# Seven products for eight in part of the MLP's second matrix, in a two-layer encoder on one core

## The chip, the core and the metric

The kernel runs on one core of a Trainium2 chip. The engines named here are TensorE (PE; its weight loads are listed as PEld), VectorE (DVE), ScalarE (ACT), GpSimd (POOL) and SyncE (SP), which issues most of the loads. Each takes its instructions in the order of a list of its own and waits where one needs another's result. The metric is the time of an execution on the device in microseconds; lower is better.

## What is computed

Two layers, 256 tokens, model width 2048. The mixer of layer 0 is a gated linear recurrence, that of layer 1 a 2-D neighbourhood attention. The part that changes is the second product of `sqrelu_mlp`.

```python
D_MODEL = 2048
SEQ = 256
D_FF = 4 * D_MODEL

def sqrelu_mlp(h, w1, w2):
    a = jax.nn.relu(h @ w1)
    return (a * a) @ w2

    for i in range(DEPTH):
        ...
        h = h + mix
        h = h + sqrelu_mlp(rms_norm(h, norm_mlp[i]), mlp_w1[i], mlp_w2[i])
        gate = jax.nn.sigmoid(rms_norm(h, norm_ple[i]) @ ple_w_gate[i])
        h = h + gate * (p[i] @ ple_w_proj[i])
    return rms_norm(h, norm_final)
```

## The kernel before

All matrix products are in float32 made of two parts: a number is split into a high part (rounded to TensorE's fp32r format) and the remainder, its low part. A product is then three matmuls: high by high, low activation by high weight, high activation by low weight. A tile of activations holds both parts side by side, 256 tokens high and 256 low. Weights come from memory as raw f32, a quarter (512 rows by 512 columns, 1 MB) at a time, and are split on the chip in halves of 128x1024 elements (`block`): ScalarE copies the half into `wh`, VectorE subtracts and writes `wl`. `wh` and `wl` have four buffers each, raw weights three, and in the MLP and gate stages two more (`phase("mlp", 2)`). One half is a step; after each step `tick` gives a turn to work that was put off (norms, transposes of the residual stream).

The MLP of a layer goes in four rounds, `for f in range(4)`. A round takes 2048 of the 8192 hidden columns: four groups of w1 (`group`, 512 columns each, weights stationary, 8 steps of 16 matmuls), each followed by relu and square and a split into a tile of activations `acts[g]`; and then w2's four column groups (`residual`, `tgroup`, `tadd`, `tproduct`), each over the round's four quarters of w2's rows. In `tproduct` the activations are stationary and the weights move: a step is 12 matmuls of 512 columns, six for each half of the tokens (s = 0, 1), and a column group is 8 steps, 96 matmuls. `residual_add` then multiplies the product by the squared norm factor r2 and adds it into the residual h (L361); in the last round `settle` squares the new h for the next norm and transposes it for the gate stage (`turned`, `gained`).

Products accumulate in PSUM in three double banks (`mm`, 2x512 columns) and two single ones (`psm`, for transposes and small products). The order of work on an engine is fixed when the program is built: a scheduler interleaves the instructions along their dependencies, by their order in the code and its own idea of when each can start.

Low products of w1: in a `group` the low products of weights stand behind the two high ones of each 128-column tile in layer 0 (`lows` = 1), behind those of all four tiles in layer 1 (`lows` = 2), and alternate with the high ones in the attention stage (`lows` = 0).

Of the kernel before, what the change touches and what calls it, by code (L numbers as in the profile page):

```python
# [12 lines left out]
F32 = mybir.dt.float32  # L13
F32R = mybir.dt.float32r
AF = mybir.ActivationFunctionType
ALU = mybir.AluOpType
# [3 lines left out]
P = 128  # L20
D = 2048
T = 256
# [8 lines left out]
V_MIX, V_MLP, V_PLE, V_FIN, V_CW, V_CB, V_AB, V_XB, V_LAM = 0, 2, 4, 6, 7, 11, 12, 14, 16  # L31
# [2 lines left out]
AHEAD = 400  # L34
LEAD = 3
NG = D // 512


class Late:


    def __init__(self, tiles):
        self.tiles = tiles
# [8 lines left out]
class Trunk:  # L52
    def __init__(self, ctx, tc, d):
        self.tc, self.nc, self.d = tc, tc.nc, d
        nc = self.nc
        pool = lambda name, bufs, **kw: ctx.enter_context(tc.tile_pool(name=name, bufs=bufs, **kw))
        self.const = pool("const", 1)
        self.state = pool("state", 1)
        self.wraw = pool("wraw", 3)
        self.wsplit = pool("wsplit", 4)  # L60
        self.work = pool("work", 2)
        self.psum = pool("psum", 3, space=PSUM)
        self.psm = pool("psm", 2, space=PSUM)
# [10 lines left out]
        self.lows = 0  # L74

    def v(self, which, c):
        i = which * NC + c
# [82 lines left out]
    def add(self, ps, w, xs, quarters, before=None, loads=1, summed=False):  # L160
        nc = self.nc

        def lows(step, ts):
            k0, wh, wl = step
            for t in ts:
                o = ps[t // 2][:, t % 2, :]
                c = slice(t * P, (t + 1) * P)
                for k in range(2):
                    kc = k0 + k
                    nc.tensor.matmul(o[:, T:], wl[:, k, c], xs[kc][:, :T], start=False, stop=kc == len(xs) - 1)  # L170
# [61 lines left out]
    def norm_begin(self):  # L232
        self.ss = self.work.tile([P, 2, NG], F32, name="ss")

# [92 lines left out]
    def load_h(self):  # L327
        nc = self.nc
        self.x = [self.state.tile([P, 4, T], F32, name=f"x{g}", tag=f"as{g}") for g in range(4)]
        self.h = [self.state.tile([P, 2, 512], F32, name=f"h{g}") for g in range(NG)]  # L330
        self.xs = self.new_xs("xs")
        self.load_pair(0)

        def squares():
            self.norm_begin()
            for _ in range(3):
                yield
            for g in range(NG):
                nc.sync.dma_start(self.h[g], self.d["h"][:, :, 512 * g : 512 * (g + 1)])
# [119 lines left out]
    def rg_mixer(self):  # L459
        nc = self.nc  # L460
        with self.phase("rg", 0) as pool:
# [31 lines left out]
            self.xs = self.new_xs("xs")  # L493
            for g in range(NG):
                if g < LEAD:
# [99 lines left out]

    def mlp_ple(self, layer, home, other, which):

        with self.phase("mlp", 2) as pool:
            self.mlp(pool, layer, home, other)
            self.lows = 0  # L600
            self.ple(pool, layer, which, other)

    def mlp(self, pool, layer, home, other):
        nc = self.nc
        r2 = pool.tile([P, 2], F32, name="r2")
        self.lows = 1 + layer
        self.ple_load(pool, layer)
        self.norm_later(lambda r: nc.vector.tensor_tensor(r2, r, r, ALU.mult))
# [27 lines left out]
    def ple(self, pool, layer, which, home):  # L636
        nc = self.nc
        r = pool.tile([P, 2], F32, name="r_ple")
        self.norm_later(lambda tok: nc.vector.tensor_copy(r, tok))
        xs = self.xlist(self.xs)  # L640
        if which is not None:
            self.xs = self.new_xs(home)
        else:
            gain = pool.tile([P, D], F32, name="gain")
            nc.scalar.dma_start(gain, self.d["gain"])
        for g in range(NG):
            if g % 2 == 0:
                halves = self.block(self.d["proj"][layer, g // 2])
            wh, wl = (t.rearrange("p (k n) -> p k n", k=2) for t in next(halves))
            pj = pool.tile([P, 2, 512], F32, name="pj", bufs=2)  # L650
# [127 lines left out]
```

## Time and profile before

| | us |
|---|---|
| median of three runs | 2349.58 |
| lowest and highest | 2348.42 to 2349.86 |
| profiled execution | 2348.25 |
| its span, first to last instruction | 2346.2 |

The span is what the trace covers; 2.05 us of the profiled execution lie around it. The mean granted clock of TensorE in it is 0.997 of full speed. In the rows below a line begins with the start and the duration where it is from a timeline; "x2" says that two like instructions were merged, and their duration is then that of both. L107 is the subtraction of the low part, L106 the copy of the high part, L361 the addition into h, L144, L145 and L149 the three kinds of matmul in w2, L183 and L170 those of w1.

### The profile page before, as it was taken

The numbers are of one execution on the slowest core, as the hardware profiler recorded it, in microseconds if no ns is written. First come the engines' busy times: TensorE is split into PE (matmuls) and PEld (weight loads), VectorE is DVE, ScalarE is ACT, GpSimd is POOL, SyncE is SP. The second block draws the span as 40 slices with busy tenths as digits, with TensorE's granted clock in tenths as the row PEclk, the third lists the DMA queues.
The fourth block names the chain that finished last, engine by engine and source line by source line (L and its number), as shares of the span: only waits on it lengthen the run. The fifth ranks groups of instructions, "written<-read, shape, count | busy, mean of one in ns | idle before, by whom it ended". The sixth has DMA issues, their size and how long they took to land.

```text
span 2346.2 us, 30442 instructions
## 1 busy us (share of the span) xinstructions
PE 2315.7 (99%) x12356; PEld 1991.8 (85%) x12356; DVE 1420.1 (61%) x1634; ACT 1177.4 (50%) x1527; POOL 0.9 (0%) x9
## 2 busy tenths in 40 slices
PE   8999999999999999999999999999999999999997
PEld 8999888888888888888888888888888888888885
DVE  6888766556555555556676666555555555555564
ACT  7888554344344344455455545544344344344453
POOL 0000000000000000000000000000000000000000
PEclk9999999999999999999999999999999999999998
DMA  7455655555555555554555555555555555555452
GB/s 289 166 177 180 229 184 186 196 190 187 197 188 189 197 187 191 191 185 163 177 178 177 179 186 220 182 195 185 192 197 183 195 191 187 196 188 189 179 181 88
DMA packets 63947, 440.93 MB, mean 188 GB/s; under 512 B 6976, under 2 KB 7104, under 8 KB 11968
## 3 DMA queue, kind: packets, MB, share of 16 engines
q1 hardware_dynamic: 62400, 433.61, 52.2%
q10 hardware_dynamic: 1408, 5.39, 0.7%
q8 instruction: 96, 1.57, 0.3%
q14 instruction: 43, 0.35, 0.0%
HBM read 436.88 MB, written 2.10 MB: 187 GB/s over the span
## 4 chain that ended last, share of the span: by engine, by line
PE 93%; ACT 3%; DVE 3%; issue 1%; DMA 0%; SPq 0%; ACTq 0%
PE mm L183 25%; PE mm L144 16%; PE mm L145 16%; PE mm L149 16%; PE mm L170 10%; PE mm L185 3%; ACT wh L106 1%; PE mm L209 1%; PE mm L207 1%; PE mm L208 1%; DVE wl L107 1%; PE pt L296 1%; DVE ig L447 1%; ACT L226 1%; ACT m L226 1%
## 5 line engine op out<-in xcount | busy, mean ns | idle before, releaser
L107 DVE TENSOR_TENSOR wl<-raw,wh 128x1024 fp32r<-128x1024 f32 x816 | 996.7, 1223 | 786.1 <-ACT wh L106 784.0
L106 ACT CAST wh<-raw 128x1024 fp32r<-128x1024 f32 x816 | 855.3, 1050 | 1004.6 <-PE mm L145 521.7
L183 PE MATMUL mm<-as,wh 128*128 128x512 f32 x1536 | 444.0, 395 | 0.0
L144 PE MATMUL mm<-wh,as 128*128 128x512 f32 x896 | 350.4, 391 | 0.0
L145 PE MATMUL mm<-wh,as 128*128 128x512 f32 x896 | 349.1, 390 | 0.0
L183 PEld LDWEIGHTS mm<-as,wh 128*128 128x128 f32 x1536 | 278.3, 189 | 53.7
L183 PE MATMUL mm<-xs,wh 128*128 128x512 f32 x1024 | 322.1, 396 | 0.0
L144 PE MATMUL mm<-wh,xs 128*128 128x512 f32 x768 | 301.0, 392 | 0.0
L145 PE MATMUL mm<-wh,xs 128*128 128x512 f32 x768 | 299.2, 390 | 0.0
L149 PE MATMUL mm<-wl,as 128*128 128x512 f32 x896 | 241.2, 390 | 0.0
L170 PEld LDWEIGHTS mm<-xs,wl 128*128 128x128 f32 x1024 | 192.4, 188 | 45.3
L149 PE MATMUL mm<-wl,xs 128*128 128x512 f32 x768 | 205.8, 389 | 0.0
L170 PE MATMUL mm<-xs,wl 128*128 128x256 f32 x1024 | 201.2, 278 | 0.0
L144 PEld LDWEIGHTS mm<-wh,as 128*128 128x128 f32 x896 | 168.3, 188 | 34.5
L145 PEld LDWEIGHTS mm<-wh,as 128*128 128x128 f32 x896 | 168.3, 188 | 34.0
L149 PEld LDWEIGHTS mm<-wl,as 128*128 128x128 f32 x896 | 167.7, 188 | 34.4
L149 PEld LDWEIGHTS mm<-wl,xs 128*128 128x128 f32 x768 | 144.1, 188 | 30.2
L144 PEld LDWEIGHTS mm<-wh,xs 128*128 128x128 f32 x768 | 144.3, 188 | 29.4
L145 PEld LDWEIGHTS mm<-wh,xs 128*128 128x128 f32 x768 | 144.3, 188 | 29.3
L183 PEld LDWEIGHTS mm<-xs,wh 128*128 128x128 f32 x1024 | 156.3, 189 | 0.3
L170 PEld LDWEIGHTS mm<-as,wl 128*128 128x128 f32 x1024 | 144.0, 190 | 12.9
L207 PE MATMUL mm<-xs,wh 128*128 128x256 f32 x512 | 146.1, 286 | 8.3 <-ACT wh L106 7.3
(140 smaller groups left out, 2119.8 us busy)
## 6 DMA issues: line engine op xcount, KB each, us to landing
raw<-in_w SPq DMA_DIRECT2D x256, 1024.0 KB, 4.7
raw<-in_qkv SPq DMA_DIRECT2D x48, 1024.0 KB, 4.8
raw<-in_ple SPq DMA_DIRECT2D x32, 1024.0 KB, 4.7
raw<-in_w_in SPq DMA_DIRECT2D x28, 1024.0 KB, 4.8
raw<-in_w_out SPq DMA_DIRECT2D x16, 1024.0 KB, 4.8
raw<-in_na_out SPq DMA_DIRECT2D x16, 1024.0 KB, 4.8
raw<-in_w_in SPq DMA_DIRECT2D x8, 512.0 KB, 8.5
raw<-in_gates SPq DMA_DIRECT2D x4, 1024.0 KB, 4.7
```

What stands on the lines that cost most here:

```text
L106: nc.scalar.copy(wh, raw[:, c])
L107: nc.vector.tensor_tensor(wl, raw[:, c], wh.bitcast(F32), ALU.subtract)
L144: nc.tensor.matmul(ps[:, s, :], part(k, 0), wh[:, k, :], start=first and k == 0, stop=False)
L145: nc.tensor.matmul(ps[:, s, :], part(k, T), wh[:, k, :], start=False, stop=False)
L149: nc.tensor.matmul(ps[:, s, :], part(k, 0), wl[:, k, :], start=False, stop=last and k == n - 1)
L170: nc.tensor.matmul(o[:, T:], wl[:, k, c], xs[kc][:, :T], start=False, stop=kc == len(xs) - 1)
L183: nc.tensor.matmul(o, wh[:, k, c], xs[kc], start=first, stop=False)
L185: nc.tensor.matmul(o[:, T:], wl[:, k, c], xs[kc][:, :T], start=False, stop=last)
L207: nc.tensor.matmul(o, a, x[:, :T], start=first, stop=False)
L208: nc.tensor.matmul(o, a, x[:, T:], start=False, stop=False)
L209: nc.tensor.matmul(o, b, x[:, :T], start=False, stop=last)
L226: self.tc.stamp_issue_order_token(self.nc.scalar.activation(*args, **kw).ins, "table")
```

## The change

A quarter of w2's rows and a pass of two neighbouring column groups (g and g + 1) make a block of 512 rows by 1024 columns. With the rows halved (k = 0, 1), the columns halved (f = 0, 1) and the tokens halved (s = 0, 1), it is eight products of blocks. In some quarters the change makes seven, by Strassen's scheme in Winograd's form: P1, Q5, P6, Q3, P2, Q4, P7 in the code. Its factors are sums of blocks. Sums of activations are made once per quarter (`seven`: the tile d, split into b, besides the plain parts in a); sums of weights are made in each pass by VectorE, in place, in the order u += r, u += v, u += w_, v += r, where u, r, v and w_ are the four blocks of the quarter, loaded apart (512 KB each). Each sum is split again (`cut`) for its product. `SEVEN = (2, 1, 2, 1)` is the number of such quarters in the four rounds. The other quarters stay as they were (`plain`) and are put between the products by the table `SPREAD`. The results go into h in pieces (`take`): P1, Q5, P6 and P7 reach more than one block of h, through a tile t of sums.

A pass uses four double banks of PSUM where there are three: P6 and P7 come into that of P1 and Q5. The MLP phase loses the two more raw buffers and gains single tiles u_w, v_w, r_w (r_w shares its place with e of `seven`). The low products of w1 and of the attention's q and k all take the order that layer 0's w1 had. The gain vector of the last norm takes the place of xs0.

```diff
+SPREAD = {1: (2, 4, 0, 0, 0, 4, 2), 2: (2, 2, 0, 0, 0, 2, 2), 3: (1, 1, 0, 0, 0, 1, 1)}
+SEVEN = (2, 1, 2, 1)
...
-                        if not self.lows:
-                            nc.tensor.matmul(o[:, T:], wl[:, k, c], xs[kc][:, :T], start=False, stop=last)
-                if self.lows == 1:
-                    lows(step, (t,))
-            if self.lows == 2:
-                lows(step, ts)
+                if not summed:
+                    for k in range(2):
+                        kc = k0 + k
+                        nc.tensor.matmul(o[:, T:], wl[:, k, c], xs[kc][:, :T], start=False, stop=kc == len(xs) - 1)
...
-        with self.phase("mlp", 2) as pool:
+        with self.phase("mlp", 0) as pool:
...
+                if g < SEVEN[f]:
+                    acts.append(self.seven(pool, ps, f"{other}{g}", g))
+                    continue
...
-            self.residual(w, self.xlist(acts), V_PLE + layer, home, by=r2, last=f == 3)
+            if f == 3:
+                self.norm_begin()
+                self.xs = self.new_xs(home)
+            for g in range(0, NG, 2):
+                self.double(pool, w, acts, SEVEN[f], g, r2, nr2)
+                if f == 3:
+                    self.settle(g, V_PLE + layer, self.xs[g])
+                    self.settle(g + 1, V_PLE + layer, self.xs[g + 1])
+    def seven(self, pool, ps, name, g):
...
+        e = pool.tile([P, 2, 2, 2, P], F32, name="e", tag="r")
+        d = pool.tile([P, 3, 2, P], F32, name="d")
+        for i in range(2):
+            u = self.joined(ps[i], "u")
+            nc.vector.scalar_tensor_tensor(e[:, i].rearrange("p k s n -> p k (s n)"), u, 0.0, u, ALU.max, ALU.mult)
+        a11, a21, a12, a22 = (e[:, i, :, s] for i in range(2) for s in range(2))
+        nc.vector.tensor_tensor(d[:, 1], a11, a21, ALU.subtract)
+        nc.vector.tensor_tensor(a21, a21, a22, ALU.subtract)
+        nc.vector.tensor_tensor(d[:, 0], a21, a11, ALU.subtract)
+        nc.vector.tensor_tensor(d[:, 2], a12, d[:, 0], ALU.add)
+        a = self.state.tile([P, 8, T], F32R, name=name)
+        b = pool.tile([P, 6, T], F32R, name=f"b{g}")
+        for o, x in ((a, e.rearrange("p i k s n -> p (i k s) n")), (b, d.rearrange("p i k n -> p (i k) n"))):
+            nc.scalar.copy(o[:, :, :P], x)
+            nc.vector.tensor_tensor(o[:, :, P:], x, o[:, :, :P].bitcast(F32), ALU.subtract)
...
+    def cut(self, src):
...
+            nc.scalar.copy(wh, src)
+            nc.vector.tensor_tensor(wl, src, wh.bitcast(F32), ALU.subtract)
...
+    def double(self, pool, w, acts, n, g, by, nby):
...
+        for pair in ("P1", "Q5"), "YZ", "WV", ("P6", "P7"):
+            ps = self.psum.tile([P, 2, 512], F32, name="mm", tag="mm")
...
+        for q in range(n):
+            nc.sync.dma_start(u[:, q, :], wide(q, 0, 0))
+        r_ = pool.tile([P, 2, 1024], F32, name="r_w", tag="r")
+        for q in range(n):
+            nc.sync.dma_start(r_[:, q, :], wide(q, 1, 0))
+        for q in range(n):
+            nc.sync.dma_start(v[:, q, :], wide(q, 1, 1))
...
+        def one(b, a, src, stop):
+
+            wh, wl = self.cut(src)
+            for k in range(2):
+                mm(b, a[:, k, :P], wh[:, k, :])
+                mm(b, a[:, k, P:], wh[:, k, :])
+            for k in range(2):
+                mm(b, a[:, k, :P], wl[:, k, :], stop and k == 1)
...
+        def take(b, f, s, sign=1):
+            h = self.h[g + f][:, s, :]
+            r = (by if sign > 0 else nby)[:, s : s + 1]
+            nc.vector.scalar_tensor_tensor(h, bank[b] if b else t, r, h, ALU.mult, ALU.add)
...
+        order = ["P1", "Q5", "P6", "Q3", "P2", "Q4", "P7"]
+        gaps = SPREAD[n]
+        for name, m in zip(order, gaps):
+            for q in range(n):
+                a = acts[q]
+                if name == "P1":
+                    one("P1", a[0], u[:, q, :], q == n - 1)
+                    nc.vector.tensor_tensor(u[:, q, :], u[:, q, :], r_[:, q, :], add)
+                elif name == "Q3":
+                    one("W", a[6], v[:, q, :], left["W"] == 1)
+                    done("W")
+                    nc.vector.tensor_tensor(v[:, q, :], v[:, q, :], r_[:, q, :], add)
+                elif name == "Q5":
+                    one("Q5", a[1], u[:, q, :], q == n - 1)
+                    nc.vector.tensor_tensor(u[:, q, :], u[:, q, :], v[:, q, :], add)
+                elif name == "P6":
...
+                    one("P6", a[4], u[:, q, :], q == n - 1)
+                    nc.vector.tensor_tensor(u[:, q, :], u[:, q, :], w_[:, q, :], add)
+                elif name == "P2":
+                    one("Y", a[2], w_[:, q, :], left["Y"] == 1)
+                    done("Y")
+                elif name == "P7":
+                    one("P7", a[5], v[:, q, :], q == n - 1)
+                else:
+                    one("Z", a[3], u[:, q, :], left["Z"] == 1)
+                    done("Z")
+                self.tick()
...
+            some(m)
```

What stands where on the engines is shown at two places, both in w2 of the third round of layer 0, where two quarters go by seven products; the number behind a name tells one buffer from another. On VectorE before, between the additions into h of the third and the fourth column group, there are the eight splits of a column group:

```order
L361 SCALAR_TENSOR_TENSOR h2_91<-mm_7004,r2_3357,h2_91 128x512 x2
L107 TENSOR_TENSOR wl_7197<-raw_7178,wh_7196 128x1024
L107 TENSOR_TENSOR wl_7215<-raw_7212,wh_7214 128x1024
L107 TENSOR_TENSOR wl_7231<-raw_7212,wh_7230 128x1024
L107 TENSOR_TENSOR wl_7249<-raw_7246,wh_7248 128x1024
L107 TENSOR_TENSOR wl_7265<-raw_7246,wh_7264 128x1024
L107 TENSOR_TENSOR wl_7287<-raw_7284,wh_7286 128x1024
L107 TENSOR_TENSOR wl_7299<-raw_7284,wh_7298 128x1024
L107 TENSOR_TENSOR wl_7329<-raw_7326,wh_7328 128x1024
L361 SCALAR_TENSOR_TENSOR h3_92<-mm_7143,r2_3357,h3_92 128x512 x2
```

In the changed program VectorE has this, in the second pass, from the splits for P6 to those for P2 (u_w, v_w and r_w are blocks of weights, raw_7331 holds the block w_, h2 and h3 are the pass's two column groups):

```order
L661 TENSOR_TENSOR wl_7335<-u_w_7206,wh_7334 128x1024
L661 TENSOR_TENSOR wl_7346<-u_w_7206,wh_7345 128x1024
L762 TENSOR_TENSOR u_w_7206<-u_w_7206,raw_7331 128x1024 x2
L661 TENSOR_TENSOR wl_7359<-v_w_7207,wh_7358 128x1024
L661 TENSOR_TENSOR wl_7370<-v_w_7207,wh_7369 128x1024
L779 TENSOR_TENSOR t_7205<-mm_7204,t_7205 128x512
L752 TENSOR_TENSOR v_w_7207<-v_w_7207,r_w_7210 128x1024
L717 SCALAR_TENSOR_TENSOR h3_92<-t_7205,nr2_3361,h3_92 128x512
L752 TENSOR_TENSOR v_w_7207<-v_w_7207,r_w_7210 128x1024
L661 TENSOR_TENSOR wl_7381<-raw_7331,wh_7380 128x1024
L661 TENSOR_TENSOR wl_7391<-raw_7331,wh_7390 128x1024
```

Sums of weights (L762, L752) and additions (L779, L717) now stand between the splits, and two of the four sums lie ahead of the splits for P2.

On TensorE before, the fourth column group goes on step by step, low products behind the high ones of the same step:

```order
L144 MATMUL mm_7143<-wh_7162,as0_6156 128x512
L145 MATMUL mm_7143<-wh_7162,as0_6156 128x512
L149 MATMUL mm_7143<-wl_7163,as0_6156 128x512 x4
L144 MATMUL mm_7143<-wh_7180,as1_6341 128x512
L145 MATMUL mm_7143<-wh_7180,as1_6341 128x512
```

In the changed program TensorE has this in the same second pass, from P2 (as0 and as1 with wh_7380 and wh_7390) on:

```order
L688 MATMUL mm_7202<-wh_7380,as0_6319 128x512 x4
L688 MATMUL mm_7202<-wl_7381,as0_6319 128x512 x2
L688 MATMUL mm_7202<-wh_7390,as1_6511 128x512 x4
L688 MATMUL mm_7202<-wl_7391,as1_6511 128x512 x2
L688 MATMUL mm_7203<-wh_7424,as2_6687 128x512 x6
L688 MATMUL mm_7202<-wh_7401,as0_6319 128x512 x4
L688 MATMUL mm_7202<-wl_7402,as0_6319 128x512 x2
L688 MATMUL mm_7202<-wh_7411,as1_6511 128x512 x4
L688 MATMUL mm_7202<-wl_7412,as1_6511 128x512 x2
L688 MATMUL mm_7203<-wh_7424,as2_6687 128x512 x2
L688 MATMUL mm_7203<-wl_7425,as2_6687 128x512 x4
```

Six high products of the plain quarter as2 were moved ahead of Q4 (wh_7401, wh_7411), and their low ones (wl_7425) behind it.

## Rows read from the trace of the kernel before

**Rows 1.** The page's head: span, then busy time, share and instructions of each engine.

```profile
span 2346.2 us, 30442 instructions
PE 2315.7 (99%) x12356; PEld 1991.8 (85%) x12356; DVE 1420.1 (61%) x1634; ACT 1177.4 (50%) x1527; POOL 0.9 (0%) x9
```

**Rows 2.** The page's chain that ended last: share of the span by engine.

```profile
PE 93%; ACT 3%; DVE 3%; issue 1%; DMA 0%; SPq 0%; ACTq 0%
```

**Rows 3.** The list of waits: engine and line, releaser, us in total, times, longest.

```profile
DVE wl L107 <- ACT wh L106: 784.0, 632, 3.0
ACT wh L106 <- PE mm L145: 521.7, 324, 2.6
DVE h L361 <- PE mm L149: 42.2, 32, 1.3
```

**Rows 4.** VectorE's timeline, w2, layer 0's third round: start, us, instruction, idle before.

```profile
781.56 1.41 DVE L361 SCALAR_TENSOR_TENSOR h<-mm,r,h 128x512 f32<-128x512 f32 x2 [1.32 <-PE mm L149]
782.88 1.21 DVE L107 TENSOR_TENSOR wl<-raw,wh 128x1024 fp32r<-128x1024 f32 x1
...
803.32 1.41 DVE L361 SCALAR_TENSOR_TENSOR h<-mm,r,h 128x512 f32<-128x512 f32 x2 [1.32 <-PE mm L149]
```

**Rows 5.** w1, w2 of that round: PE, PEld, DVE, ACT, POOL, clock, DMA, GB/s.

```profile
670.40:759.60 89.20, 89.20 (x514) 77.84 (x513) 52.22 (x53) 39.57 (x46) 0.00 (x0) 1.00 0.53 186
759.60:846.60 87.00, 87.00 (x386) 72.09 (x385) 46.25 (x44) 35.82 (x36) 0.00 (x0) 1.00 0.56 196
```

**Rows 6.** Timeline of VectorE where it is dense, in the RG-LRU stage.

```profile
87.11 1.20 DVE L107 TENSOR_TENSOR wl<-raw,wh 128x1024 fp32r<-128x1024 f32 x1
88.23 1.22 DVE L451 TENSOR_TENSOR ig<-ig,ig 128x1024 f32<-128x1024 f32 x1
89.37 0.68 DVE L392 TENSOR_TENSOR xr<-mm,rstd 128x512 f32<-128x512 f32 x1
```

**Rows 7.** Timeline of VectorE in w1 of layer 0's third round.

```profile
736.72 0.69 DVE L221 TENSOR_TENSOR u<-mm,low 128x512 f32<-128x512 f32 x1
737.44 0.69 DVE L617 SCALAR_TENSOR_TENSOR u<-u 128x512 f32<-128x512 f32 x1
...
739.49 0.68 DVE L214 TENSOR_TENSOR as<-u,as 128x512 fp32r<-128x512 f32 x1
740.09 0.68 DVE L221 TENSOR_TENSOR u<-mm,low 128x512 f32<-128x512 f32 x1
...
759.01 0.69 DVE L221 TENSOR_TENSOR u<-mm,low 128x512 f32<-128x512 f32 x1
```

**Rows 8.** ScalarE's costliest group: instruction, count, busy us, mean ns, idle.

```profile
L106 ACT CAST wh<-raw 128x1024 fp32r<-128x1024 f32 x816 | 855.3, 1050 | 1004.6 <-PE mm L145 521.7 <-PE mm L183 354.2 <-issue 90.2
```

**Rows 9.** Timeline of TensorE where the same round goes from w1 to w2.

```profile
759.59 0.40 PE L144 MATMUL mm<-wh,as 128*128 128x512 f32 x1
```

**Rows 10.** Timeline of VectorE where a column group settles, gate stage of layer 0.

```profile
1033.11 0.48 DVE L286 SCALAR_TENSOR_TENSOR xs<-pt,vec,xs 128x256 fp32r<-128x256 f32 x1
1034.14 0.48 DVE L286 SCALAR_TENSOR_TENSOR xs<-pt,vec,xs 128x256 fp32r<-128x256 f32 x1 [0.54 <-ACT xs L285]
```

**Rows 11.** Timeline of VectorE at the ends of two w1 groups, layer 1.

```profile
1744.36 1.28 DVE L221 TENSOR_TENSOR u<-mm,low 128x512 f32<-128x512 f32 x2
...
1766.73 1.28 DVE L221 TENSOR_TENSOR u<-mm,low 128x512 f32<-128x512 f32 x2
```

**Rows 12.** Timeline of TensorE in a group of the attention stage.

```profile
1158.61 0.40 PE L183 MATMUL mm<-as,wh 128*128 128x512 f32 x1
...
1162.77 0.40 PE L183 MATMUL mm<-as,wh 128*128 128x512 f32 x1
```

**Rows 13.** DMA issues (KB each, us to landing), and SP's longest wait.

```profile
raw<-in_w SPq DMA_DIRECT2D x256, 1024.0 KB, 4.7
raw<-in_w_in SPq DMA_DIRECT2D x8, 512.0 KB, 8.5
...
SPq L99 <- DVE wl L107: 2017.0, 385, 11.2
```

More of the change, by code (lines that the diff above doesn't have):

```diff
@@ L161, in add @@
         nc = self.nc
[L163 to L170, printed above, removed]
         def tiles(step, ts):
@@ L605, in mlp, with then @@
         r2 = pool.tile([P, 2], F32, name="r2")
-        self.lows = 1 + layer
         self.ple_load(pool, layer)
-        self.norm_later(lambda r: nc.vector.tensor_tensor(r2, r, r, ALU.mult))
+        nr2 = pool.tile([P, 2], F32, name="nr2")
+        def then(r):
+            nc.vector.tensor_tensor(r2, r, r, ALU.mult)
+            nc.vector.tensor_scalar_mul(nr2, r2, -1.0)
+        self.norm_later(then)
         xs = self.xlist(self.xs)
@@ new lines, in seven @@
+    def seven(self, pool, ps, name, g):
+        nc = self.nc
+        e = pool.tile([P, 2, 2, 2, P], F32, name="e", tag="r")
[13 more added lines that the diff above has]
+            nc.vector.tensor_tensor(o[:, :, P:], x, o[:, :, :P].bitcast(F32), ALU.subtract)
+        a = a.rearrange("p (i k s) n -> p i s k n", i=2, k=2)
+        b = b.rearrange("p (i k) n -> p i k n", i=3)
+        return [a[:, i, s] for i in range(2) for s in range(2)] + [b[:, i] for i in range(3)]
@@ new lines, in cut, with mm, plain, done @@
+    def cut(self, src):
+        nc = self.nc
+        wh = self.wsplit.tile([P, 1024], F32R, name="wh")
+        wl = self.wsplit.tile([P, 1024], F32R, name="wl")
+        with self.tc.high_priority(self.ahead):
+            nc.scalar.copy(wh, src)
+            nc.vector.tensor_tensor(wl, src, wh.bitcast(F32), ALU.subtract)
+        return (t.rearrange("p (k n) -> p k n", k=2) for t in (wh, wl))
+    def double(self, pool, w, acts, n, g, by, nby):
+        nc = self.nc
+        add = ALU.add
+        bank = {}
+        for pair in ("P1", "Q5"), "YZ", "WV", ("P6", "P7"):
+            ps = self.psum.tile([P, 2, 512], F32, name="mm", tag="mm")
+            for i, b in enumerate(pair):
+                bank[b] = ps[:, i, :]
+        t = self.work.tile([P, 512], F32, name="t", tag="low")
+        wide = lambda q, f, k: w(g + f)[q][:, 1024 * k : 1024 * (k + 1)]
+        u = pool.tile([P, 2, 1024], F32, name="u_w")
+        v = pool.tile([P, 2, 1024], F32, name="v_w")
+        for q in range(n):
[5 more added lines that the diff above has]
+            nc.sync.dma_start(v[:, q, :], wide(q, 1, 1))
+        w_ = None
+        begun = set()
+        def mm(b, x, y, stop=False):
+            nc.tensor.matmul(bank[b], x, y, start=b not in begun, stop=stop)
+            begun.add(b)
+        def one(b, a, src, stop):
[5 more added lines that the diff above has]
+                mm(b, a[:, k, :P], wl[:, k, :], stop and k == 1)
+        def plain(f, q, k):
+            wh, wl = self.cut(raws[f, q][:, 1024 * k : 1024 * (k + 1)])
+            xs = [acts[q][:, 2 * k + j, :] for j in range(2)]
+            for s in range(2):
+                b = ("YZ", "WV")[f][s]
+                for j in range(2):
+                    mm(b, xs[j][:, s * P : (s + 1) * P], wh[:, j, :])
+                    mm(b, xs[j][:, T + s * P : T + (s + 1) * P], wh[:, j, :])
+            for s in range(2):
+                b = ("YZ", "WV")[f][s]
+                for j in range(2):
+                    mm(b, xs[j][:, s * P : (s + 1) * P], wl[:, j, :], left[b] == 1 and j == 1)
+        def take(b, f, s, sign=1):
+            h = self.h[g + f][:, s, :]
+            r = (by if sign > 0 else nby)[:, s : s + 1]
+            nc.vector.scalar_tensor_tensor(h, bank[b] if b else t, r, h, ALU.mult, ALU.add)
+        rest = [(f, q, k) for f in range(2) for q in range(n, 4) for k in range(2)]
+        raws = {}
+        left = {"Y": n + len(rest) // 2, "Z": n + len(rest) // 2, "W": n + len(rest) // 2, "V": len(rest) // 2}
+        home = {"Y": (0, 0), "Z": (0, 1), "W": (1, 0), "V": (1, 1)}
+        def done(b):
+            left[b] -= 1
+            if not left[b]:
+                take(b, *home[b])
+        def some(m):
+            for _ in range(m):
+                if rest:
+                    f, q, k = rest.pop(0)
+                    if k == 0:
+                        raws[f, q] = self.raw()
+                        nc.sync.dma_start(raws[f, q], w(g + f)[q])
+                    plain(f, q, k)
+                    for b in ("YZ", "WV")[f]:
+                        done(b)
+                    self.tick()
[15 more added lines that the diff above has]
+                elif name == "P6":
+                    if w_ is None:
+                        w_ = self.raw().rearrange("p (q n) -> p q n", q=2)
+                        for i in range(n):
+                            nc.sync.dma_start(w_[:, i, :], wide(i, 0, 1))
+                    one("P6", a[4], u[:, q, :], q == n - 1)
[8 more added lines that the diff above has]
+                    done("Z")
+                self.tick()
+            if name == "P1":
+                take("P1", 0, 0)
+                nc.scalar.copy(t, bank["P1"])
+            elif name == "Q5":
+                take("Q5", 1, 0)
+                take("Q5", 1, 1)
+            elif name == "P6":
+                nc.vector.tensor_tensor(t, bank["P6"], t, add)
+                take(None, 1, 0, -1)
+            elif name == "P7":
+                nc.vector.tensor_tensor(t, bank["P7"], t, add)
+                take(None, 0, 1)
+                take(None, 1, 1, -1)
+            some(m)
+        assert not rest and not any(left.values())
@@ L643, in ple @@
         else:
-            gain = pool.tile([P, D], F32, name="gain")
+            gain = self.state.tile([P, D], F32, name="gain", tag="xs0")
             nc.scalar.dma_start(gain, self.d["gain"])
@@ L649, in ple @@
             wh, wl = (t.rearrange("p (k n) -> p k n", k=2) for t in next(halves))
-            pj = pool.tile([P, 2, 512], F32, name="pj", bufs=2)
+            pj = pool.tile([P, 2, 512], F32, name="pj")
             pp = [self.psm.tile([P, 512], F32, name="pp", tag="psm") for _ in range(2)]
```

2 lines of the change are left out of this document (removed).

## The prediction

> **What bounds the kernel now.** I read the page's totals first: TensorE is busy for 2315.7 of a span of 2346.2 us and VectorE for 1420.1 [rows 1]. Busy matmuls overlap, so the share alone proves little; the chain that ended last says it better: 93% of it lies on TensorE, 3% on VectorE and 3% on ScalarE [rows 2]. The list of waits confirms the direction: VectorE waits 784.0 us for ScalarE's high parts, ScalarE waits 521.7 us for TensorE to free a buffer of weights, and even the additions of w2 into h (L361) sit 1.3 us each before a product ends [rows 3]. So TensorE sets the pace, and the others wait for it. The stage that changes is w2. There, one column group of 96 matmuls takes from 781.56 to 803.32, which is 21.76 us or 226.7 ns for a matmul of 512 columns [rows 4]. In the w2 stage of the third round of layer 0 (87.0 us) TensorE is busy throughout, VectorE for 46.25 and ScalarE for 35.82 [rows 5]. VectorE's 41 spare microseconds there are what the change spends.
>
> **What is removed.** I call the work of `double` on two column groups a pass. Each quarter of w2 that goes by seven products loses one product of eight in each pass: six matmuls of 48. A layer has 2+1+2+1 = 6 such quarters and two passes for each, so 24 cases in both layers, 144 matmuls, each worth 226.7 ns since TensorE is the bound: **-32.6 us**, if nothing else becomes late. Passes come in two kinds. A heavy pass (rounds 1 and 3 of a layer) has two quarters by seven products: 180 matmuls, 40.8 us. A light pass (rounds 2 and 4) has one: 186 matmuls, 42.2 us. Both were 192, 43.5 us.
>
> **What VectorE gets.** A split is one VectorE instruction of 128x1024. In a dense stretch such instructions start 1.12 to 1.14 us apart, and a plain f32 sum of the same size (L451) is followed after 1.14 us, although one lasts 1.22 [rows 6]. I take 1.14 for each split and each sum of weights. An addition into h costs 0.66 (two start at 781.56, the next work at 782.88 [rows 4]). A dependent 512-column operation follows after 0.72, an independent one after 0.60 [rows 7]. A quarter by seven products needs 7 splits and 4 sums per pass, one by eight needs 4 splits; each pass has ten additions into h and two sums into t. Heavy pass: 30 x 1.14 + 10 x 0.66 + 2 x 0.60 = 42.0 us of VectorE against 40.8 of TensorE. Light pass: 23 x 1.14 + 7.8 = 34.0 against 42.2. So light passes keep TensorE as the bound, and **heavy passes put VectorE level with it**. ScalarE, with 22 copies of 1.05 us and one of t in a heavy pass, is far from it [rows 8].
>
> **How much of that TensorE feels.** VectorE may run ahead by four weight buffers, and its additions into h wait for TensorE, so a surplus is not saved up. I walked a heavy round along VectorE's order. It takes up the last w1 product 0.58 us before w1 ends (759.01 against the first w2 matmul at 759.59 [rows 7, 9]); by then the first two splits, their sums and a third split are done, because w1 leaves it time. From there to the split for the second pass's last P2 product (the last row of its fence above) stand 33 splits, 14 sums, 14 additions into h, 3 sums into t and six operations on the w1 product: 53.6 + 9.2 + 1.8 + 3.9 = 68.5 us, so it ends 68.0 us after w1 (0.1 for the last write). TensorE wants that split after a first pass of 40.8 us and 106 matmuls (24.0 us), at 64.8. The difference, 3.2 us per heavy round, is the floor of the stall: nothing of this stream can be skipped. Some eight of these instructions use a result of the one before them and cost 0.12 more (0.72 against 0.60 [rows 7]), which makes 4.2. The matmuls drawn ahead of Q4 (TensorE's fence) shift the stall but do not shorten VectorE's stream. Behind the last P2 the splits thin out and VectorE recovers. Four heavy rounds: **+16.8 us**, with 12.8 as the lower end; the upper end is a spacing equal to the duration, 1.22: 0.08 x 64 = 5.1 more per round, +37.
>
> The trace shows starts closer together than a duration [rows 6]. The Trainium skill ("VectorE: DVE Perf Modes", section "The DRAIN you can't avoid") says that the next operation does not start until the pipe is empty; by that rule the upper end would hold, which is the first rival below.
>
> **Smaller terms.** In a light round the second pass's plain products need the bank of W and V, whose two additions (1.32 us and a start) come after the last product, while only P1 (1.36 us) covers them: 0.3 us in each of four rounds, **+1.2**, between 0 and 1 per light pass. At the end of each layer's w2, two column groups settle together instead of one: four transposes, then ScalarE and VectorE by turns. VectorE's part of such a pair recurs every 1.03 us [rows 10], so two groups through two small banks need about 3 to 4 us, against 5 us of matmuls that TensorE's order puts between in the second pass and 2.7 us in the gate stage. I take 0.5 at four places, **+2.0**, bounds 0 and 6. The order of low products changes in two stages. A layer-1 w1 group takes 22.37 us now and a layer-0 group, whose order all get, 22.29 [rows 7, 11], so 16 groups gain about 1.2. In the attention stage a step takes 2.773 (twelve pairs from 1158.61 to 1162.77 [rows 12]), and with layer 0's order 22.29 / 8 = 2.786, so 64 steps lose 0.8. I set this to zero. `seven` adds some 2.5 us of VectorE to a w1 group in a stage where it is busy for 52.22 of 89.20 us [rows 5]; the cover is the three splits by which it is ahead. The gain vector now waits for xs0; ScalarE issues it after its last split for P7, when TensorE is past Q4, so nothing queues behind it.
>
> **Loads.** The bytes are the same. Raw buffers fall from five to three, the blocks u, v and r have one buffer each, and SP issues in order. A load lands in 4.7 us, and SP's waits are for VectorE's splits, 11.2 us at worst [rows 13]. The tight one is u of a second pass: it can be issued only when Q4's split has read it, and its first split can start some 7 us later, a few microseconds before TensorE needs it. I cost it at nothing; late loads are the second rival.
>
> **Sum.** -32.6 + 16.8 + 1.2 + 2.0 = -12.6 us. The profiled execution took 2348.25 us (2.05 around the span), so 2335.65; the median of the three runs, 2349.58, lies 1.33 above that execution, so **2337.0 us**, 0.5% faster.
>
> **Rivals.** (1) VectorE is the plain bound of heavy rounds. If its operations start a full duration apart (many wait for ScalarE or for their own engine), a heavy round loses 9.3 us and not 4.2: 2337.0 + 4 x 5.1 = **2357.4**, slower. It decides from a spacing of about 1.19 on, where the 3.1 us that a heavy round keeps are gone. Against it stand the dense rows [rows 6], for it that the additions there depend on one another more than in those rows. (2) Late loads: if u lands after 8.5 us, as loads of 512 KB did at the program's start [rows 13], each of eight second passes waits about 1.5 us: +12, **2349**, no change. For it: one buffer each, one queue in order. Against it: the engines of the DMA are busy 0.56 of that stage [rows 5], and the start of the program is its densest. (3) The sums hide after all and all of 32.6 us is gained: **2317.0**. Against it: the floor of 3.2 us per heavy round.
>
> **How the numbers follow.** Forecast (from 2328 to 2344) 0.54; rival 1 0.16; rival 2 0.20; rival 3 0.10. A difference of 0.2% (4.7 us) is about what a measurement of this kernel can tell from no change. Faster by more: forecast and rival 3, 0.64. Within: rival 2, 0.20. Slower: rival 1, 0.16. The range runs from 2328, which is the lower end of the heavy term with no smaller term (2329.8) and a little for the order of low products, to 2353, which takes in rival 2 and heavy rounds of about 8 us; left out are rival 3 and the worse half of rival 1.
>
> **What would show it.** TensorE should have 144 matmuls fewer and idle gaps of 3 to 5 us per heavy round, released by the split's VectorE instruction and lying between Q3 and Q4; light rounds should be nearly without. VectorE should run without a pause through a heavy round, with splits and sums 1.14 apart. A heavy round's w2 should last 85.8 us and a light one's 84.7, against 87.0. I am wrong if light passes show gaps, if TensorE waits for a DMA through a late high part, if the spacing is 1.2 or more, or if VectorE is idle in heavy passes while TensorE is too: then the order of the engines, not VectorE's load, decides.

## The result and the profile after

The changed kernel takes 2331.39 us (median of four runs, 2330.6 to 2331.89), the kernel before 2349.55 beside it: a ratio of 0.9923, 95% interval 0.9906 to 0.9940, which is 18.2 us. The forecast was 2337.0, and 2331.39 lies inside its range. The profiled execution took 2331.45 us with a span of 2329.7, 16.5 us less than the span before [rows 1].

The page's head of the changed kernel (span; busy time, share and instructions by engine; then shares of the chain that ended last, by engine):

```profile
span 2329.7 us, 30727 instructions
...
PE 2288.6 (98%) x12212; PEld 1959.5 (84%) x12212; DVE 1712.8 (74%) x1980; ACT 1265.8 (54%) x1615; POOL 0.9 (0%) x9
...
PE 89%; DVE 6%; ACT 3%; issue 2%; DMA 0%; SPq 0%; ACTq 0%
```

TensorE has 144 instructions fewer, VectorE 346 more. VectorE's share of the chain went from 3% [rows 2] to 6%. Stretches of the changed kernel, with the columns of [rows 5]: first round's w2 of layer 0 (heavy), second round's w2 (light), third round's w2 (heavy), fourth round's w2 (light, with the settling behind it):

```profile
407.64:493.48 85.84, 83.31 (x363) 67.34 (x362) 83.89 (x86) 49.08 (x50) 0.00 (x0) 1.00 0.50 179
582.64:667.54 84.90, 84.90 (x374) 69.70 (x373) 70.86 (x73) 43.16 (x44) 0.00 (x0) 1.00 0.59 214
...
756.70:842.56 85.86, 83.34 (x362) 67.33 (x361) 83.89 (x86) 49.03 (x50) 0.00 (x0) 1.00 0.49 179
...
931.72:1018.46 86.74, 86.74 (x391) 71.37 (x390) 73.59 (x81) 49.44 (x64) 0.00 (x0) 1.00 0.50 176
```

In a heavy round VectorE is busy for 83.89 of 85.84 us, where it was busy for 46.25 of 87.00 [rows 5], and TensorE is no longer busy throughout. A light round, with 12 matmuls more, is about 0.95 us shorter than a heavy one, and TensorE has no gap in it.

This is how the stall looks. The timeline of VectorE in the second pass of the third round, from the sums of Q5 to the splits for P2 (start, duration, instruction, idle before), and then that of TensorE, first from Q3 on in the first pass and then at P2 of the second:

```profile
806.70 2.36 DVE L755 TENSOR_TENSOR u_w<-u_w,v_w 128x1024 f32<-128x1024 f32 x2
808.97 2.36 DVE L661 TENSOR_TENSOR wl<-raw,wh 128x1024 fp32r<-128x1024 f32 x2
811.24 1.41 DVE L717 SCALAR_TENSOR_TENSOR h<-mm,r,h 128x512 f32<-128x512 f32 x2
812.56 2.35 DVE L661 TENSOR_TENSOR wl<-u_w,wh 128x1024 fp32r<-128x1024 f32 x2
814.83 2.36 DVE L762 TENSOR_TENSOR u_w<-u_w,raw 128x1024 f32<-128x1024 f32 x2
817.10 2.36 DVE L661 TENSOR_TENSOR wl<-v_w,wh 128x1024 fp32r<-128x1024 f32 x2
...
822.90 2.36 DVE L661 TENSOR_TENSOR wl<-raw,wh 128x1024 fp32r<-128x1024 f32 x2
```

```profile
779.71 0.74 PE L688 MATMUL mm<-wl,b 128*128 128x512 f32 x2 [0.48 <-DVE wl L661]
780.84 0.73 PE L688 MATMUL mm<-wl,as 128*128 128x512 f32 x2 [0.39 <-DVE wl L661]
...
784.91 1.21 PE L688 MATMUL mm<-wh,as 128*128 128x512 f32 x4 [0.16 <-DVE h L717]
...
821.62 1.08 PE L688 MATMUL mm<-wh,as 128*128 128x512 f32 x4
824.18 0.73 PE L688 MATMUL mm<-wl,as 128*128 128x512 f32 x2 [1.48 <-DVE wl L661]
```

VectorE goes without a pause. Pairs of 128x1024 start 2.27 us apart, 1.135 for one. In the second pass TensorE has done the four high products of P2 and stands for 1.48 us until the low part of the same weights is there. The list of waits of TensorE, w2 alone (us in total, times, longest):

```profile
PE mm L688 <- DVE wl L661: 9.4, 12, 1.5
...
PE mm L688 <- DVE h L717: 0.7, 4, 0.2
```

No wait of TensorE for a DMA stands in that list. The 9.4 us are less than the heavy rounds lose, since idle time is not all that a wait costs: at the idle of 1.48 the next matmul starts 2.56 us after the first of the four, where four take 0.91, so 1.65 us late.

### The profile page after: what moved, and what is told of

Read it like the earlier page. It is cut to its first block, busy times and chain, and to the rows that moved or that the text cites. A ratio compares the mean times of both kernels' runs of the same rounds, so it can differ in the third digit from the quotient of the medians.

```text
span 2329.7 us, 30727 instructions
## 1 busy us (share of the span) xinstructions
PE 2288.6 (98%) x12212; PEld 1959.5 (84%) x12212; DVE 1712.8 (74%) x1980; ACT 1265.8 (54%) x1615; POOL 0.9 (0%) x9
## 4 chain that ended last, share of the span: by engine, by line
PE 89%; DVE 6%; ACT 3%; issue 2%; DMA 0%; SPq 0%; ACTq 0%
PE mm L175 26%; PE mm L688 25%; PE mm L179 13%; PE mm L145 6%; PE mm L146 6%; PE mm L150 6%; DVE wl L661 2%; ACT wh L107 1%; PE mm L199 1%; PE mm L197 1%; PE mm L198 1%; DVE wl L108 1%; PE pt L286 1%; DVE v_w L752 1%; DVE ig L437 1%
## 5 line engine op out<-in xcount | busy, mean ns | idle before, releaser
L108 DVE TENSOR_TENSOR wl<-raw,wh 128x1024 fp32r<-128x1024 f32 x560 | 682.8, 1223 | 447.2 <-ACT wh L107 444.4
L179 PEld LDWEIGHTS mm<-as,wl 128*128 128x128 f32 x1536 | 288.3, 188 | 67.6
L179 PE MATMUL mm<-as,wl 128*128 128x256 f32 x1536 | 302.2, 278 | 0.0
L661 DVE TENSOR_TENSOR wl<-raw,wh 128x1024 fp32r<-128x1024 f32 x184 | 221.6, 1221 | 29.8 <-ACT wh L660 29.2
L688 PE MATMUL mm<-wh,as 128*128 128x512 f32 x832 | 210.0, 390 | 0.3 <-DVE h L717 0.3
L688 PE MATMUL mm<-wh,xs 128*128 128x512 f32 x832 | 210.0, 390 | 0.3 <-DVE h L717 0.3
L179 PE MATMUL mm<-xs,wl 128*128 128x256 f32 x1024 | 201.2, 278 | 0.0
L688 PEld LDWEIGHTS mm<-wh,as 128*128 128x128 f32 x832 | 155.4, 188 | 34.5 <-DVE h L717 2.2
L688 PEld LDWEIGHTS mm<-wh,xs 128*128 128x128 f32 x832 | 155.4, 188 | 34.4 <-DVE h L717 2.2
L197 PE MATMUL mm<-xs,wh 128*128 128x256 f32 x512 | 146.2, 286 | 8.5 <-ACT wh L107 7.4
L145 PE MATMUL mm<-wh,as 128*128 128x512 f32 x384 | 150.4, 392 | 0.0
L146 PE MATMUL mm<-wh,as 128*128 128x512 f32 x384 | 149.7, 390 | 0.0
L660 ACT CAST wh<-u_w 128x1024 fp32r<-128x1024 f32 x96 | 100.4, 1050 | 89.4 <-PE mm L688 54.4
L199 PE MATMUL mm<-xs,wl 128*128 128x256 f32 x512 | 145.6, 286 | 0.7 <-DVE wl L108 0.6
L198 PE MATMUL mm<-xs,wh 128*128 128x256 f32 x512 | 145.5, 284 | 0.0
```

The costliest lines, as they stand in the source:

```text
L108: nc.vector.tensor_tensor(wl, raw[:, c], wh.bitcast(F32), ALU.subtract)
L145: nc.tensor.matmul(ps[:, s, :], part(k, 0), wh[:, k, :], start=first and k == 0, stop=False)
L146: nc.tensor.matmul(ps[:, s, :], part(k, T), wh[:, k, :], start=False, stop=False)
L197: nc.tensor.matmul(o, a, x[:, :T], start=first, stop=False)
L198: nc.tensor.matmul(o, a, x[:, T:], start=False, stop=False)
L199: nc.tensor.matmul(o, b, x[:, :T], start=False, stop=last)
```

## The experiments

Each run is compared with the kernel before on the same chip. The first matmul of layer 0's w1 comes between 316.8 and 318.3 us in the runs, which has nothing to do with w2, so I read single effects from the stages in the trace.

**Light rounds only.**

```diff
-SEVEN = (2, 1, 2, 1)
+SEVEN = (1, 1, 1, 1)
```

> One quarter by seven products in every round instead of 2, 1, 2, 1. Theory (VectorE's load sets the heavy rounds): rounds 1 and 3 become light ones, w2 85.85 -> 84.9 us although they do 12 more matmuls each; four rounds, -3.8 us against the changed kernel, about 2327.6, with no TensorE wait of more than 0.5 us in any round. Rival A (the gain follows the number of products, heavy passes are worth their 40.8 us): 48 matmuls more than the changed kernel, 48 x 226.7 ns = +10.9 us, 2342.3.

Measured: 2327.52 us, ratio 0.9909 (0.9894 to 0.9924), 3.9 us faster than the changed kernel though it has 48 matmuls more. Read from the stages it is 3.6: the four rounds that lasted 85.83 to 85.86 take 84.93 to 85.00 here. The third round's w2:

```profile
755.17:840.14 84.97, 84.97 (x374) 69.71 (x373) 70.85 (x73) 43.19 (x44) 0.00 (x0) 1.00 0.57 201
```

TensorE is busy throughout, and waits for no split in w2. Rival A, by which the number of products decides, is 15 us off.

**Heavy rounds only.**

```diff
-SEVEN = (2, 1, 2, 1)
+SEVEN = (2, 2, 2, 2)
```

> Two quarters by seven products in every round. Theory (VectorE's load): rounds 2 and 4 become heavy ones, w2 84.9 -> 85.85, +0.95 each, four rounds +3.8 us, about 2335.2. Rival A (number of products): 48 matmuls fewer, -10.9 us, 2320.5.

Measured: 2339.03 us, ratio 0.9958 (0.9944 to 0.9972): 48 matmuls fewer than the changed kernel and 7.6 us slower. The sign is the theory's, the size twice it. The second rounds cost 1.3 and 1.0 us more, as expected. The fourth rounds cost 2.3 and 2.6 more, beyond what the theory had; VectorE also has the settling to do there. The fourth round's w2 of layer 0:

```profile
933.45:1022.66 89.21, 86.28 (x379) 68.88 (x378) 87.25 (x94) 56.01 (x70) 0.00 (x0) 1.00 0.42 154
```

The next stage's first matmul starts at 1022.50 (the row ends with the last record of w2), so w2 lasts 89.05 instead of 86.74, with VectorE busy for 87.25.

**Sums over 64 columns.** The four sums of `double` get an end, so that every instruction stays but sums take little time:

```diff
+        m_ = 64 if n == 2 else 1024
...
-                    nc.vector.tensor_tensor(u[:, q, :], u[:, q, :], r_[:, q, :], add)
+                    nc.vector.tensor_tensor(u[:, q, :m_], u[:, q, :m_], r_[:, q, :m_], add)
...
```

> In heavy passes each sum of weights is made over 64 of its 1024 columns only (the rest of each sum is left out), so that every instruction stays, in nearly the same order, but the sums take next to no time of VectorE. Theory (load): 14 sums of 1.14 us leave the stream ahead of the last P2, the floor is gone, heavy w2 falls from 85.85 to about 82.1 us (81.6 of matmuls and the 0.5 that light rounds lose); four rounds, -15 us, about 2316.4. Rival B (the chains split, product, order of the engines and banks set the 4.25 us): most of the gaps stay, heavy w2 84 or more, time above 2324.

Measured: 2317.26 us, ratio 0.9864 (0.9849 to 0.9879). The third round's w2:

```profile
753.88:836.15 82.27, 82.27 (x362) 67.61 (x361) 71.13 (x86) 49.06 (x50) 0.00 (x0) 1.00 0.51 187
```

3.6 of the 4.25 us that a heavy round loses against its 81.6 us of matmuls go when the sums take no time, with the same number of instructions in nearly the same order. So it is the time of the sums. A sum is also a link in the chain to its own split and product, so this run alone does not tell VectorE's load from that chain; the next one bears on it. The 0.66 left is no wait for VectorE. Part of it shows in TensorE's timeline of this run, with a product of a plain activation block and then one of a sum of blocks (`b`):

```profile
763.41 1.07 PE L688 MATMUL mm<-wh,as 128*128 128x512 f32 x4
764.31 0.61 PE L688 MATMUL mm<-wl,as 128*128 128x512 f32 x2
764.77 1.98 PE L688 MATMUL mm<-wh,as 128*128 128x512 f32 x8
...
770.21 1.10 PE L688 MATMUL mm<-wh,b 128*128 128x512 f32 x4
771.15 0.62 PE L688 MATMUL mm<-wl,b 128*128 128x512 f32 x2
771.61 1.10 PE L688 MATMUL mm<-wh,b 128*128 128x512 f32 x4
```

The six matmuls with `as` take 1.36 us (763.41 to 764.77), the six with `b` 1.40. A heavy round has twelve products with `b`, 0.5 us. Why they are slower stays open.

**One more VectorE instruction.**

```diff
                     nc.vector.tensor_tensor(u[:, q, :], u[:, q, :], w_[:, q, :], add)
+                    nc.vector.tensor_tensor(u[:, q, :], u[:, q, :], u[:, q, :], ALU.max)
```

> One more VectorE instruction of 128x1024 (a maximum of the sum with itself, in place, exact) behind each sum u += w_, not needed before Q4: four in a heavy round, all ahead of the second pass's last P2 split, two in a light round. Theory (load): a heavy round's w2 grows by 4 x 1.14 = 4.6 us (5.0 if each adds the 0.12 of a dependent operation) to 90.4 to 90.9, a light round's not at all (34.0 + 1.1 us of VectorE a pass against 42.2): four heavy rounds, +18 to +20 us, 2349.6 to 2351.6. Rival B (chains and order, not load): an instruction that no product waits for costs at most 1 us a round, below 2336.

Measured: 2347.52 us, ratio 0.9994 (0.9985 to 1.0004), 16.1 us more than the changed kernel. In the four heavy rounds the w2 grew by 3.9, 3.6, 3.7 and 5.2 us. The last of these holds more than VectorE's load: behind three waits of TensorE of 0.38, 1.27 and 0.39 us its granted clock fell from 1.00 to 0.50 (1.2 GHz) for 3.41 us, columns as in [rows 5]:

```profile
2034.40:2037.81 3.41, 3.41 (x9) 2.63 (x8) 2.34 (x3) 1.06 (x2) 0.00 (x0) 0.50 0.37 72
```

The other three rounds give 0.93 us for each instruction, under the 1.14 expected. The light rounds stayed at 84.91. The same instruction costs nothing in one kind of round and most of its spacing in the other, though no matmul but those of the later Q4 needs it: VectorE's load is the bound of the heavy rounds.

**Plain steps earlier.**

```diff
-SPREAD = {1: (2, 4, 0, 0, 0, 4, 2), 2: (2, 2, 0, 0, 0, 2, 2), 3: (1, 1, 0, 0, 0, 1, 1)}
+SPREAD = {1: (2, 4, 0, 0, 0, 4, 2), 2: (3, 3, 0, 0, 0, 1, 1), 3: (1, 1, 0, 0, 0, 1, 1)}
```

> In heavy passes the plain steps (12 matmuls for one split) are put 3, 3, 0, 0, 0, 1, 1 behind P1 ... P7 instead of 2, 2, 0, 0, 0, 2, 2: two more of them stand ahead of the second pass's last P2. Nothing is added or left out. Theory (load, and where it stands): to the last P2 VectorE then has 2 x 1.14 us more, TensorE 24 matmuls (5.4 us) more, so the 4.25 us at that place fall to about 1, and the round ends near 82.5 to 83.5 us instead of 85.85; four heavy rounds, -10 to -13 us, 2318 to 2321. Rival C (the 3.2 us are a floor that no order of the same work can remove, as the prediction says): heavy w2 stays above 84.8, time above 2327.

Measured: 2322.65 us, ratio 0.9888 (0.9873 to 0.9903), 8.7 us faster than the changed kernel with the same work. Heavy rounds took 83.7, 83.8, 84.2 and 83.6 us. Rival C is out, and with it my word "floor": VectorE's stream to the last P2 can't be skipped, but what TensorE has to do beside it can be made longer. The gain is 2 us a round where I expected 2.4 to 3.4. The one wait left in the third round is at the same place:

```profile
825.28 0.73 PE L688 MATMUL mm<-wl,as 128*128 128x512 f32 x2 [1.13 <-DVE wl L661]
```

**A sum on GpSimd.**

```diff
-                    nc.vector.tensor_tensor(v[:, q, :], v[:, q, :], r_[:, q, :], add)
+                    (nc.gpsimd if n == 2 else nc.vector).tensor_tensor(v[:, q, :], v[:, q, :], r_[:, q, :], add)
```

> In heavy passes the sum v += r (needed only by P7) is made by GpSimd, four of a heavy round's sixteen sums. Theory (load): 4 x 1.14 = 4.6 us leave VectorE's stream ahead of the last P2, the 4.25 us go, heavy w2 82 to 82.5; -14 us, about 2318. Rival D (GpSimd and VectorE disturb each other, or GpSimd is so slow that P7 waits for v): VectorE's instructions last longer beside GpSimd's, or a gap opens at P7; heavy w2 84 or more, 2325 or above.

Measured: 2352.35 us, ratio 1.0018 (1.0008 to 1.0027), 21 us slower than the changed kernel. Taking four sums of a heavy round from VectorE made that round 5.0 to 5.3 us longer. The timeline of GpSimd in the third round, and then that of VectorE beside its first two sums:

```profile
781.40 2.41 POOL L752 TENSOR_TENSOR v_w<-v_w,r_w 128x1024 f32<-128x1024 f32 x1 [301.51 <-DVE wl L661]
784.97 2.81 POOL L752 TENSOR_TENSOR v_w<-v_w,r_w 128x1024 f32<-128x1024 f32 x1 [1.16 <-DVE wl L661]
```

```profile
780.05 1.22 DVE L661 TENSOR_TENSOR wl<-v_w,wh 128x1024 fp32r<-128x1024 f32 x1
...
782.05 2.84 DVE L661 TENSOR_TENSOR wl<-v_w,wh 128x1024 fp32r<-128x1024 f32 x1
784.81 0.74 DVE L717 SCALAR_TENSOR_TENSOR h<-t,nr,h 128x512 f32<-128x512 f32 x1
785.48 4.52 DVE L661 TENSOR_TENSOR wl<-raw,wh 128x1024 fp32r<-128x1024 f32 x2
```

The split beside GpSimd's sum lasts 2.84 us instead of 1.22, the two beside the next one 4.52 instead of 2.36. So each sum moved away costs VectorE 1.6 to 2.2 us, and saves 1.14. TensorE then waits up to 2.3 us at one split. The first half of rival D is what happened; v was not late for P7. Not all of the loss is VectorE's: in each of the four heavy rounds, and in none of the changed kernel's, the granted clock of TensorE falls to 0.50 for 3.41 us behind such a wait. TensorE in the third round, and then the stretch at the lower clock, columns as in [rows 5]:

```profile
834.38 0.72 PE L688 MATMUL mm<-wl,as 128*128 128x512 f32 x2 [2.27 <-DVE wl L661]
834.95 3.81 PE L688 MATMUL mm<-wh,as 128*128 128x512 f32 x9
838.59 0.63 PE L688 MATMUL mm<-wl,as 128*128 128x512 f32 x2
```

```profile
835.13:838.54 3.41, 3.41 (x9) 2.65 (x9) 3.41 (x5) 0.33 (x1) 0.00 (x0) 0.50 0.94 317
```

The nine matmuls take 3.64 us (834.95 to 838.59) instead of 2.04, so by this estimate 1.6 us of a round's loss, 6.4 of the 21, are the clock. The Trainium skill ("SBUF — State Buffer", section "SBUF: two separate sides") says that a VectorE operation with two SBUF inputs and a GpSimd operation that reads SBUF exclude each other for a whole instruction; the 2.84 us agree with that, since the split ends 1.08 us after GpSimd's sum, at 784.89 against 783.81.

**The order of low products alone**, in the kernel before (`lows` 1 in every stage):

```diff
-            self.lows = 0
+            self.lows = 1
...
-        self.lows = 1 + layer
+        self.lows = 1
```

> The kernel before with the low products behind each 128-column tile wherever a group is used, which is the part of the change outside w2, alone. By the prediction's estimate layer-1 w1 gains 1.2 us and the attention stage loses 0.8: 0 to -0.5 us against the kernel before. If the 1.1 us that the gate and attention stretch lost in the changed kernel come from this order, the stretch from layer 0's w2 to layer 1's w1 is shorter here too, and the whole is -2 to -2.5 us; if they come from settling, it is not.

Measured: 2344.73 us, ratio 0.9983 (0.9974 to 0.9992), 4.3 us faster than before, more than either answer above; the prediction had put this term at zero. The attention stage and a w1 stage of layer 1, before and then in this run, columns as in [rows 5]:

```profile
1128.11:1520.76 392.65, 392.08 (x2083) 332.02 (x2082) 254.93 (x343) 201.39 (x295) 0.00 (x0) 1.00 0.53 189
1698.16:1787.63 89.47, 89.47 (x513) 78.60 (x512) 51.33 (x52) 39.59 (x45) 0.00 (x0) 1.00 0.54 189
```

```profile
1127.83:1518.45 390.62, 390.00 (x2084) 331.22 (x2082) 255.08 (x343) 201.67 (x295) 0.00 (x0) 1.00 0.53 189
1695.58:1784.74 89.16, 89.16 (x513) 77.80 (x512) 52.22 (x53) 39.54 (x46) 0.00 (x0) 1.00 0.53 186
```

Attention gains 2.0 us where I had a loss of 0.8. The changed kernel has the same 390.60. TensorE's timeline of the kernel before, in a later group of that stage than the one of [rows 12], and the same stretch of this run:

```profile
1230.03 0.40 PE L183 MATMUL mm<-as,wh 128*128 128x512 f32 x1
...
1234.27 0.40 PE L183 MATMUL mm<-as,wh 128*128 128x512 f32 x1
```

```profile
1230.44 0.62 PE L183 MATMUL mm<-as,wh 128*128 128x512 f32 x2
...
1234.62 0.62 PE L183 MATMUL mm<-as,wh 128*128 128x512 f32 x2
```

Twelve pairs of a high and a low product took 4.24 us here before, 4.16 in [rows 12], and 4.18 in the new order. The stage has eight such groups of 128 matmuls. I had taken my step from the second of them; the first two had the 4.16, the six others the 4.24. Why the first two were faster I don't know.

**Plain steps between P6 and Q3.**

```diff
-SPREAD = {1: (2, 4, 0, 0, 0, 4, 2), 2: (2, 2, 0, 0, 0, 2, 2), 3: (1, 1, 0, 0, 0, 1, 1)}
+SPREAD = {1: (2, 4, 0, 0, 0, 4, 2), 2: (2, 2, 2, 0, 0, 1, 1), 3: (1, 1, 0, 0, 0, 1, 1)}
```

> In heavy passes the plain steps stand 2, 2, 2, 0, 0, 1, 1 behind P1 ... P7: as many ahead of the last P2 as with 3, 3, 0, 0, 0, 1, 1, but two of them between P6 and Q3. If only the sum of VectorE's and TensorE's work ahead of the last P2 counts, heavy w2 is the same 83.7 us and the time the same 2322.7 us. If it matters that VectorE can be ahead by no more than four buffers (a dense stretch of products then spends what it has, and plain steps ahead of it can't be saved up), the shorter dense stretches give 82.8 to 83.4 us, 2319 to 2321.5.

Measured: 2321.31 us, ratio 0.9885 (0.9870 to 0.9900). All four heavy rounds took 83.45 to 83.51, just above the second answer's 82.8 to 83.4 and 0.2 to 0.7 better than with 3, 3; the time lies inside the second answer. So the sum of the work ahead of the last P2 tells most of the gain over the changed kernel. The four buffers would explain the rest, but no run tests them by themselves.

**Three heavy rounds**, with that order:

```diff
-SEVEN = (2, 1, 2, 1)
+SEVEN = (2, 2, 2, 1)
```

> Plain steps 2, 2, 2, 0, 0, 1, 1 with 2, 2, 2, 1. The same -2.2 us or more against the run with 2, 1, 2, 1 and this order; 2317 to 2320.5.

Measured: 2318.68 us (2318.28 to 2319.5), ratio 0.9875 (0.9858 to 0.9891), 0.5% faster than the changed kernel, 2.6 us faster than the same order with 2, 1, 2, 1, as expected, and the fastest of those that compute all. The third round's w2:

```profile
752.45:835.89 83.44, 82.97 (x362) 67.42 (x361) 82.16 (x85) 48.78 (x50) 0.00 (x0) 1.00 0.48 172
```

TensorE is busy for 82.97 of 83.44 us and VectorE for 82.16: both are at their end. The fourth round stays light because of the settling. With 3, 3 instead, the same three heavy rounds gave 2321.0 us, ratio 0.9883 (0.9868 to 0.9898):

> Plain steps 3, 3, 0, 0, 0, 1, 1 and two quarters by seven products in the second round too (2, 2, 2, 1). By the w2 stages measured so far a heavy round of this order takes 83.8 us and a light one 84.9: two rounds, -2.2 us against the same order with 2, 1, 2, 1, about 2320.4. If instead a heavy round after a heavy one starts without VectorE's lead, 2322 to 2324.

That is 1.7 us less than with 2, 1, 2, 1, where I expected 2.2. The heavy rounds there ranged from 83.6 to 84.6 us.

## Why the prediction came out right

The sum of the prediction and what the stages of the profiled executions show, in us (heavy and light: difference of a round's w2 to the 87.05 before, times four; in a fourth round the light round's 84.90 is taken for w2, and what is left stands under settling):

| term | forecast | measured |
|---|---|---|
| heavy rounds, 4 x (-5.4 + 4.2) | -5.0 | 4 x (85.85 - 87.05) = -4.8 |
| light rounds, 4 x (-2.7 + 0.3) | -9.7 | 4 x (84.90 - 87.05) = -8.6 |
| settling and transposes | +2.0 | -0.3 |
| order of low products | 0 | -3.2 |
| start of the program | 0 | +0.5 |
| sum (forecast: of the unrounded terms) | -12.6 | -16.4 |

**The heavy rounds** were right in kind, and by the mechanism that I gave: VectorE's stream is the bound up to the second pass's P2. The walk had VectorE's split for the last P2 end 68.0 us after w1, or some 69 with the dependent operations. In the third round w1 ends at 756.70, and the pair of P2 splits that starts at 822.90 ends at 825.26: 68.6. The spacing of 1.135 is the 1.14 of [rows 6]. The runs with short sums and with one more instruction show that it is VectorE's time. That the loss of 4.25 a round meets the 4.2 so closely is partly luck: only 3.6 of it go with the sums, between the floor of 3.2 and the 4.2, and the other 0.66 is no wait for VectorE and stood in no term; the slower products with `b` are some 0.5 of it. TensorE's idle time is 2.5 us a heavy round, not the 3 to 5 that I named as the sign. I gave the gaps no pass, and looked at the last P2 alone. They come in two places of equal size: the first pass has lost 1.65 us by 784.91 already (the three late starts from 779.71 on, against 226.7 ns a matmul; two wait for a split, the third for an addition into h), and the second pass adds 1.65 at the first of its two P2 splits, the one that TensorE waits for. The walk had one place, at the last split. That the first dense stretch uses up the lead that w1 left is my reading of the first place; no run tests it alone.

**The light rounds** were right in kind: VectorE has 14 us to spare and no gap opens. They lost 0.57 us against 372 matmuls of 226.7 ns, and not 0.3; six products with `b`, 0.04 us each, are 0.24 of it. The list of waits has none in a light round, so that the rest lies at the bank of W and V, as I had it, is not shown.

**Settling** was mis-sized, by 2.3 us. The fourth round's w2 and the gate behind it took 192.31 before and 189.97 after, 2.34 less, of which a light round is 2.15. TensorE is busy throughout that stretch, so nothing of it waited for the settling: I had priced a queue through two small banks that TensorE's other matmuls cover.

**The order of low products** was mis-sized, by 3.2 us; the w1 part (1.2) was right, and the attention part had the wrong sign, from a row that stood for two of eight groups and not for the stage.

So of the 18.2 us, 3 to 4 come from the reordered low products, not from the seven products. The forecast was 5.6 us too slow. 3.8 of that come from the terms: settling and the order of low products, 5.5 together and outside the part that I had walked most carefully, less 1.7 by which the rounds and the start gained less. The rest is no stage: I had the median 1.33 us above the profiled execution, as before the change, and it lies 0.06 below; and 1.75 us lie around the span instead of 2.05.

**Rival 1** (a spacing of 1.22) is refuted by the rows above: pairs start 2.27 apart. The rule of "The DRAIN you can't avoid" in "VectorE: DVE Perf Modes" of the Trainium skill would give 2.44; that section also excepts an operation that is not held, which starts earlier, and the 2.27 us agree with the exception and not with the rule. (The 3.1 us that the prediction lets a heavy round keep are the whole forecast gain divided by four; by its own terms a heavy round keeps 5.4 - 4.2 = 1.2.) **Rival 2** (late loads) finds no row: TensorE and ScalarE wait for no DMA in w2, and u lands after 5.3 us where the rival needs 8.5 (page of the changed kernel, KB each, median us to landing):

```profile
u_w<-in_w SPq DMA_DIRECT2D x24, 512.0 KB, 5.3
```

It was not tried by an experiment of its own. **Rival 3** (all hidden) is met by the run with short sums, 2317.26 measured against its 2317.0, but partly by chance: some 3 of that gain are the order of low products.

## What to carry to other kernels

Saving work on the engine that bounds is worth it only up to the point where the helper engine's work per stretch passes it. Here the second quarter of a pass took 12 matmuls away in a round and made that round 0.95 us longer, and doing less of it was faster until the order was mended. When two engines come level, compare their running sums up to the densest place, not their totals: moving plain steps ahead of that place gained 2.4 us a round with no work saved. An edit that looks like housekeeping (the order of low products) deserves its own run, and a rate taken from one row should be looked up in another group of the same stage first.

## What the runs showed that I had not expected

- GpSimd is no free helper for VectorE's sums: beside a sum of 128x1024 on GpSimd (2.4 to 2.8 us), a split of VectorE lasted 2.84 us instead of 1.22.
- A wait of TensorE can cost more than its own length: with the sums on GpSimd the granted clock fell from 1.00 to 0.50 for 3.41 us once in every heavy round, behind waits of up to 2.3 us, and once in the run with one more instruction, behind waits of up to 1.27; in the changed kernel, with waits of up to 1.48, it stayed at 1.00 in w2.
- The same twelve pairs of matmuls took 4.16 us in the first two groups of the attention stage and 4.24 in the other six, at a granted clock of 1.00; with low products in pairs behind high ones they took 4.18 in all eight.
- Six matmuls took 1.36 us with plain blocks of activations as stationary operand and 1.40 with sums of blocks, back to back and with no wait in the trace.
